# A streaming encoder layer whose second half reuses weight parts that the first half has made, and whose sample rows get a task of their own

## The chip, the cores and the metric

One core of one Trainium2 chip runs the whole kernel. Its engines have a queue each: TensorE (PE) does the matmuls, VectorE (DVE), ScalarE (ACT) and GpSimd (POOL) the work on elements, SyncE (SP) issues nearly all transfers (DMA). The time is the device time of one execution in microseconds, lower is better; several executions give the median. All times in this text come from one profiled execution and from the runs beside it.

## The reference

One layer for two request groups: 2048 prompt rows (new streams) and 32 sample rows (running streams), width 1024, all in float32. Cut to what matters here:

```python
h = rmsnorm(x, g_pre_mix); z = h @ w_in            # z: pool input u, and q, f, i, g of four heads
y_pool = pool_mix(u_ext, n_valid, w_pool, pool_scale)
S1, o = hgrn_run(S0, q, k, v, logf)                # recurrence by chunks
y_hg = rmsnorm(o, g_hg_norm) * silu(zg)
y_mix = concat([y_pool, y_hg]) @ w_out             # output projection
x = x + rmsnorm(y_mix, g_post_mix)
h2 = rmsnorm(x, g_pre_ffn)
f = (silu(h2 @ w_gate) * (h2 @ w_up)) @ w_down     # 1024 -> 2816 -> 1024
x = x + rmsnorm(f, g_post_ffn)
```

The outputs are both groups' rows and their new pool histories and recurrence states.

## The kernel before, in words

**A matmul.** An f32 matmul is done as three products of rounded parts: a tensor is split into `hi`, a rounded copy made by a cast on ACT, and `lo`, the rest, made by a subtraction on DVE; hi·hi, hi·lo and lo·hi are added up in PSUM. On top of this the projections work in 2x2 blocks with seven products of sums of blocks instead of eight (`PRODUCTS`, p = 1 to 7). The sums of blocks of a weight and their splits are its "forms".

**Stages.** The prompt is worked in two halves of 1024 tokens (`S.B` false and true). For each: values and front (norm, `w_in`, heads and pool), output projection (`project`), gate and up (`gate_up`), which writes the hidden rows to DRAM. `down` runs for both halves at the end. In the profiled execution the first half's front lasts until about 290 us, its projection until 374, its gate and up until 798; the second half's values until 842, front until about 1045, projection until 1141, gate and up until 1597, `down` until 2033.

**Weights of the projection.** A stream of items (`want`, `take`, L295 to L313) loads raw rows of 1024 numbers a partition (`wrow`, 512 KB) and splits each into two `whi` and two `wlo` tiles (L269, L270). `project` takes one item of two k-blocks at a time; its seven products run in the order of `PROJ`. The blocks for products 1, 2 and 3 are rows of `mixed` or `w_out`, those for 4, 5, 6 and 7 are sums that `out_forms` (L657) writes to DRAM, into `proj`, during the first half's front. Each half loads and splits all of them. The matmuls `ops` (stationary: tokens' forms `yhi`, `ylo`; moving: `whi`, `wlo`) end in a row tile `ym` per 128 tokens.

**From the projection to gate and up.** `finished` (L1530) sums the squares of half a row tile on ACT (`junk`, with a statistic in `st`; L343) and multiplies by the norm's weight on DVE (L1534). `post` (L1659) is a task for each group of four row tiles: POOL turns `st` into a reciprocal root (L347 to L354), DVE scales and adds the residual (L1693), ACT sums squares again (`junk`, 1024 wide), POOL makes a second root, the tile is scaled on DVE (L1676) or ACT (L1674), PE transposes it in quarters (`tps`, L366), and DVE and ACT take the transposes out of PSUM as `h2raw` (L373 to L377), from which `fhi` and `flo`, the tokens' forms, are made. The group of products 5 and 6 is the first, that of 2 and 3 the second. In the second half the second group has a fifth member, the 32 sample rows: matmuls `osps`, gathered into `yms` on ACT and DVE, multiplied by the norm's weight on POOL (L1578), and transposed last (`stps`, L420).

**Gate and up.** 22 column blocks of 256, `m` even for gate and odd for up. Each has seven forms `wf` (512 KB: hi and lo of 128x512) made from raw columns `wraw` (512 KB): `prep_sum`, `prep_hi` (ACT, L1847), `prep_lo` (DVE, L1852). The first six blocks (`LEAD`) are worked together product by product, in slots, since the second group of tokens is not ready at once. Both halves make all forms. The outputs in PSUM are `gx`, `gy`, `gz` and `gw`; `c` are their copies on the way to the hidden rows `hhi` and `hlo`.

**What sets the order.** PE's order is that in which the program is written. `Pace` counts the time of the matmuls written so far; a `Task` is a generator whose `yield n` says how many ns of matmuls are to pass before its next step, and `poll()` between matmuls takes the steps that are due. So the second group of transposes falls among the matmuls of gate and up where `post` is due. On DVE, ACT, POOL and SP a scheduler sets the order from its own estimate of what is ready; each of these queues is then worked strictly in that order. Tiles come from rings: 39 of 4 KB a partition (`wf`, `wraw`, `wrow`, `ym`, ...), 26 of 2 KB (`whi`, `wlo`, `c`, ...), and 8 PSUM banks, so a transfer or a matmul can also wait for the last reader of a buffer. `weight_forms` (L479) is a task that makes forms for the second half's front; what it has left is finished at the start of that half (`second_start`, L2298), ahead of its loads of `xT` and `wrow`.

## Time and profile before

| | us |
|---|---|
| median of 3 runs | 2042.76 (2042.34 to 2043.32) |
| profiled execution | 2042.75 |
| its span, first to last instruction | 2041.0 |
| PE busy | 2020.8 (99%) |
| DVE busy | 1522.4 (75%) |
| ACT busy | 900.9 (44%) |
| POOL busy | 274.1 (13%) |
| moved by DMA | 393 MB, mean 193 GB/s |

The span's mean granted clock of TensorE was 0.997. In a row of a timeline stand the start, the duration, the engine, the line, the operation and its tiles (out<-in), and in brackets the engine's idle time before it with what ended it. A matmul's duration overlaps the next one; what it costs is its distance to the next. A window row gives the stretch, its length, the busy time (and instructions) of PE, weight loads, DVE, ACT and POOL, the granted clock, the DMA engines' busy share and GB/s. A row of a group gives least, median and greatest duration in ns, and the first and last start in us.

### The profile page before, as it was taken

The page shows a single profiled execution, that of the slowest core. Times are in us where ns is not written, and L with a number is a line of the kernel's source. Part 1 is how long each engine was busy: PE and PEld are TensorE (multiplying, and loading weights), DVE is VectorE, ACT ScalarE, POOL GpSimd, SP SyncE. Part 2 cuts the span into 40 slices and gives each one's busy share as a digit, 9 for nine tenths or more (in the row PEclk, how much of TensorE's full clock was granted, in tenths as well). Part 3 has the DMA queues.
Part 4 walks back from the last instruction along what each step waited for, and adds up shares of the span by engine and source line. Part 5 has one row for each costly group of instructions (what it writes and reads, how often), then busy time and mean ns, then how long its engine had stood idle before and what let it go on. Part 6 is the DMA issues. An engine that isn't in the chain of part 4 may idle for free.

```text
span 2041.0 us, 34566 instructions
## 1 busy us (share of the span) xinstructions
PE 2020.8 (99%) x12892; PEld 1655.8 (81%) x12892; DVE 1522.4 (75%) x2515; ACT 900.9 (44%) x1800; POOL 274.1 (13%) x378
## 2 busy tenths in 40 slices
PE   9999999999999999999999999999999999999998
PEld 8888888788888888788887688888888778888876
DVE  5667678999788889666878887776676656566587
ACT  6654445864545445444456754444444411011032
POOL 0122311300000000033312300000001111010034
PEclk9999999999999999999999999999999999999999
DMA  8556333548776778745545615544455897677778
GB/s 296 181 187 218 115 113 135 186 130 250 227 238 212 228 222 253 264 160 176 168 177 180 188 53 155 165 145 144 141 149 160 252 355 215 204 228 206 216 202 217
DMA packets 434583, 393.33 MB, mean 193 GB/s; under 512 B 22680, under 2 KB 329360, under 8 KB 434416
## 3 DMA queue, kind: packets, MB, share of 16 engines
q1 hardware_dynamic: 427744, 381.11, 59.1%
q0 software_dynamic: 2016, 7.34, 2.0%
q10 hardware_dynamic: 4656, 2.67, 0.4%
q8 instruction: 102, 1.67, 0.3%
q14 instruction: 65, 0.53, 0.1%
HBM read 253.87 MB, written 137.17 MB: 192 GB/s over the span
## 4 chain that ended last, share of the span: by engine, by line
PE 90%; DVE 5%; ACT 1%; DMA 1%; POOL 1%; issue 1%; DVEq 0%; SPq 0%; ACTq 0%; POOLq 0%
PE gx L226 26%; PE gy L226 14%; PE dx L226 10%; PE mmb L226 8%; PE ops L226 6%; PE gz L226 6%; PE dy L226 5%; PE vps L226 4%; PE dz L226 3%; PE gb L226 1%; PE gw L226 1%; PE gsps L226 1%; DVE acc L2144 1%; PE ups L226 1%; DMA wraw<-in_w_up_dram 1%
## 5 line engine op out<-in xcount | busy, mean ns | idle before, releaser
L226 PE MATMUL gx<-fhi,wf 128*128 128x512 f32 x1632 | 459.5, 391 | 0.9 <-ACT c L1041 0.9
L226 PEld LDWEIGHTS gx<-fhi,wf 128*128 128x128 f32 x1632 | 304.6, 188 | 67.3 <-issue 1.6
L226 PE MATMUL gx<-flo,wf 128*128 128x512 f32 x816 | 255.3, 391 | 0.0
L226 PE MATMUL gy<-fhi,wf 128*128 128x512 f32 x832 | 239.7, 390 | 0.1
L226 PE MATMUL dx<-dhi,hst 128*128 128x512 f32 x640 | 185.4, 391 | 0.7 <-DVE acc L2144 0.7
L226 PEld LDWEIGHTS gy<-fhi,wf 128*128 128x128 f32 x832 | 155.5, 188 | 33.4 <-issue 0.9
L226 PEld LDWEIGHTS gx<-flo,wf 128*128 128x128 f32 x816 | 153.2, 188 | 31.9 <-issue 0.2
L2144 DVE TENSOR_TENSOR acc<-dx,acc 128x512 f32<-128x512 f32 x168 | 115.1, 689 | 71.4 <-PE dx L226 70.7
L1852 DVE TENSOR_TENSOR wf<-s,wf 128x512 fp32r<-128x512 f32 x176 | 120.4, 687 | 56.7 <-ACT wf L1847 55.7
L226 PEld LDWEIGHTS dx<-dhi,hst 128*128 128x128 f32 x640 | 119.6, 188 | 30.0 <-issue 3.4
L1847 ACT CAST wf<-s 128x512 fp32r<-128x512 f32 x176 | 107.7, 620 | 72.3 <-PE gy L226 27.9
L2083 ACT CAST dhi<-t 128x1024 fp32r<-128x1024 f32 x20 | 20.7, 1053 | 252.2 <-DVE dlo L2084 183.2
L226 PE MATMUL gy<-flo,wf 128*128 128x512 f32 x416 | 129.2, 390 | 0.0
L226 PE MATMUL gz<-fhi,wf 128*128 128x512 f32 x384 | 111.9, 392 | 1.0 <-ACT h2raw L375 1.0
L1847 ACT CAST wf<-wraw 128x512 fp32r<-128x512 f32 x132 | 80.7, 621 | 68.5 <-PE gx L226 38.8
L1852 DVE TENSOR_TENSOR wf<-wraw,wf 128x512 fp32r<-128x512 f32 x132 | 91.0, 694 | 18.6 <-ACT wf L1847 18.4
L226 PE MATMUL dx<-dlo,hst 128*128 128x512 f32 x320 | 98.7, 389 | 0.0
L226 PE MATMUL dy<-dhi,hst 128*128 128x512 f32 x320 | 98.5, 389 | 0.0
L226 PEld LDWEIGHTS gy<-flo,wf 128*128 128x128 f32 x416 | 78.1, 188 | 16.2
L2144 DVE TENSOR_TENSOR acc<-dy,acc 128x512 f32<-128x512 f32 x88 | 60.6, 689 | 38.6 <-PE dy L226 38.0
L226 PE MATMUL mmb<-hTlo,whi 128*128 128x512 f32 x256 | 84.6, 398 | 0.0
L226 PEld LDWEIGHTS gz<-fhi,wf 128*128 128x128 f32 x384 | 71.3, 188 | 15.6 <-ACT h2raw L375 1.2
(418 smaller groups left out, 4075.9 us busy)
## 6 DMA issues: line engine op xcount, KB each, us to landing
hst<-hdFalse SPq DMA_DIRECT2D x140, 256.0 KB, 3.1
hst<-hdTrue SPq DMA_DIRECT2D x140, 256.0 KB, 4.2
wf<-wd SPq DMA_DIRECT2D x112, 256.0 KB, 4.9
wraw<-in_w_gate_dram SPq DMA_DIRECT2D x50, 512.0 KB, 4.9
wraw<-in_w_up_dram SPq DMA_DIRECT2D x50, 512.0 KB, 4.2
hdFalse<-hhi SPq DMA_DIRECT2D x77, 256.0 KB, 2.6
hdFalse<-hlo SPq DMA_DIRECT2D x77, 256.0 KB, 2.5
hdTrue<-hhi SPq DMA_DIRECT2D x77, 256.0 KB, 2.3
```

Of the source, the lines that this page charges most:

```text
L226: nc.tensor.matmul(out, l, r, start=start, stop=stop, skip_group_check=more)
L1847: nc.scalar.copy(wf[:, 0], getattr(M, src) if isinstance(src, str) else src)
L1852: nc.vector.tensor_tensor(wf[:, 1], getattr(M, src) if isinstance(src, str) else src, wf[:, 0].bitcast(F32), ALU.subtract)
L2083: nc.scalar.copy(hi, src)
L2144: nc.vector.tensor_tensor(dst, ps, dst, ALU.add)
```

## The change

**Parts of the projection's weights.** `out_forms` now also splits: for each of four k-blocks and each of seven products, `put` casts the block or sum to `poh` on ACT and subtracts to `pol` on DVE, and stores both in DRAM (`proj`, 56 stores of 256 KB where there were 16). Both halves load them as `phi` and `plo` (`project_loads`, `project_take`), 56 + 56 loads of 256 KB each into the ring of 2 KB tiles, in place of 16 loads of 512 KB with 28 + 28 splits. The sample's projection loads its raw rows by itself.

**Kept forms.** The forms of gate and up of the first four blocks, and products 1 and 2 of blocks 4 and 5, 32 in all (`kept`), are stored by the first half when PE reaches their step (32 stores of 512 KB into `gd`), and the second half loads them into `wf` (32 loads) and neither sums nor splits. The raw columns that the sample's gate and up need are loaded when product 6 is prepared.

**The sample's own task.** `sample_post` takes the sample rows out of `post`: PSUM is copied once by ACT (`oss`), and the gathering, norms and transposes follow in a task of their own that begins 6000 ns of matmuls behind product 3 (`SAMPLE`). `post` has four members in both halves. The multiplication by the norm's weight moves from POOL to DVE.

**Later weights for the second front.** `weight_forms` begins 62000 instead of 50000 ns behind the projection.

```diff
+SAMPLE = 6000.0
+KEPT = 4
@@ project_loads @@
-        def project_loads(S):
-            def load(p, k):
...
-            for p in PROJ:
-                for k in pair_order(p):
-                    want(lambda p=p, k=k: load(p, k))
+        def project_loads(S, n):
+            forms_of_out.finish()
+            todo = [(p, k) for p in PROJ for k in pair_order(p)]
+            while len(S.pw) < min(n, len(todo)):
+                p, k = todo[len(S.pw)]
+                hl = [[t2("phi", dt=F32R), t2("plo", dt=F32R)] for _ in range(2)]
+                for kk in range(2):
+                    for i in range(2):
+                        nc.sync.dma_start(out=hl[kk][i].bitcast(F32), in_=proj[p][k + kk, :, i, :])
+                S.pw.append(hl)
+        def project_take(S, look):
+            i = S.pu
+            S.pu += 1
+            project_loads(S, i + 1 + look)
+            r = S.pw[i]
...
@@ out_forms, for each k @@
+                def put(p, src):
+                    hi, lo = t2("poh", dt=F32R), t2("pol", dt=F32R)
+                    nc.scalar.copy(hi, src)
+                    yield 2200.0
+                    v.tensor_tensor(lo, src, hi.bitcast(F32), ALU.subtract)
+                    for i, t in enumerate((hi, lo)):
+                        nc.sync.dma_start(out=proj[p][k, :, i, :], in_=t.bitcast(F32))
+                yield from put(1, b11)
+                yield from put(2, b21)
+                yield from put(3, b22)
...
-                for p, t in ((7, t3), (5, b12), (6, b22), (4, b21)):
-                    nc.sync.dma_start(out=proj[p][k * P:(k + 1) * P, :], in_=t)
+                yield from put(4, b21)
@@ project @@
                 def fetch(k, look):
-                    raw, hi, lo = take(look)
...
+                    w[k], w[k + 1] = project_take(S, look)
...
-                    S.post.append(Task(post(S, 1, yms[1], yss, sts[1]), 0.0, after=S.post[0]))
+                    S.post.append(Task(post(S, 1, yms[1], sts[1]), 0.0, after=S.post[0]))
                 if smp:
                     sample(p - 2, raws)
+                    if p == 3:
+                        S.post.append(Task(sample_post(S, yss, *rows), SAMPLE))
...
+        def sample_post(S, halves, xh, gv):
+            v = nc.vector
+            ym = [t2("yms", [NS, 512]) for _ in range(2)]
+            st = new_stat()
+            for i in range(2):
+                nc.scalar.copy(ym[i], halves[i][0:NS])
+                for q in range(1, 4):
+                    v.tensor_tensor(ym[i], halves[i][32 * q:32 * q + 32], ym[i], ALU.add)
+                sumsq(ym[i], NS, st[0:NS, i:i + 1])
+                yield 2500.0
...
+            for i in range(2):
+                v.tensor_tensor(ym[i], ym[i], gv[i], ALU.mult)
+                v.scalar_tensor_tensor(ym[i], ym[i], rs, xh[i][0:NS], ALU.mult, ALU.add)
+                nc.sync.dma_start(out=x1_rows(SEQ, NS)[:, i * 512:i * 512 + 512], in_=ym[i])
+                sumsq(ym[i], NS, st[0:NS, i:i + 1])
+                yield 2500.0
...
@@ gate_up @@
+                if S.B and m < KEPT:
+                    M.formed.update((0, 1))
+            def kept(m, p):
+                return m < KEPT or m < LEAD and p < 3
@@ load, prep_sum, prep_lo @@
+                if S.B and kept(m, p):
+                    return
@@ prep_hi @@
                 wf = M.f[p] = xtile("wf", [P, 2, 512])
+                if S.B and kept(m, p):
+                    nc.sync.dma_start(out=wf.bitcast(F32), in_=gd[m][p - 1])
+                    if p == 6:
+                        M.r = [raw_cols(M.w, (m // 2 * 2 + i) * P) for i in range(2)]
+                    return
@@ step @@
+                if kept(m, p) and not S.B:
+                    nc.sync.dma_start(out=gd[m][p - 1], in_=M.f[p].bitcast(F32))
@@ main @@
-                    forms = Task(weight_forms(), 50000.0)
+                    forms = Task(weight_forms(), 62000.0)
```

Three places where the order of instructions moves. The number behind a tile's name tells tiles apart; it is another in the two programs, and so are the line numbers.

DVE in the second half, ahead of the first group's transposes, before (row tiles of the first group: 11651, 11670, 11697, 11726; of the second: 11608, 11613, 11618):

```order
L1554 TENSOR_TENSOR ym_11608<-ops_12067,ym_11608 128x512
L1693 SCALAR_TENSOR_TENSOR ym_11726<-ym_11726,st_11506,xr_11882 128x512
L1693 SCALAR_TENSOR_TENSOR ym_11726<-ym_11726,st_11506,xr_11883 128x512
L1676 TENSOR_SCALAR ym_11651<-ym_11651,st_12054 128x1024
L1534 TENSOR_TENSOR ym_11608<-ym_11608,gv_11495 128x512
L1554 TENSOR_TENSOR ym_11613<-ops_12104,ym_11613 128x512
L270 TENSOR_TENSOR wlo_12141<-wrow_11987,whi_12140 128x512
L1554 TENSOR_TENSOR ym_11618<-ops_12148,ym_11618 128x512
```

and in the change (first group: 11811, 11830, 11855, 11874; second: 11760, 11765, 11770):

```order
L1566 TENSOR_TENSOR ym_11760<-ops_12214,ym_11760 128x512
L1730 SCALAR_TENSOR_TENSOR ym_11874<-ym_11874,st_11663,xr_12026 128x512
L1730 SCALAR_TENSOR_TENSOR ym_11874<-ym_11874,st_11663,xr_12027 128x512
L1546 TENSOR_TENSOR ym_11760<-ym_11760,gv_11652 128x512
L1714 TENSOR_SCALAR ym_11811<-ym_11811,st_12189 128x1024
L1566 TENSOR_TENSOR ym_11765<-ops_12251,ym_11765 128x512
L1566 TENSOR_TENSOR ym_11770<-ops_12295,ym_11770 128x512
```

The multiplication by `gv` of the second group's first tile has moved ahead of the scaling of the first group's first tile; the split is gone, and two additions out of PSUM follow the scaling at once. On ACT the sum of squares of that second group's tile now stands ahead of the scaling L1712, where it stood behind L1674.

PE at the start of the second half's gate and up, before (the second group's first transposes):

```order
L226 MATMUL gx_12538<-fhi_12321,wf_12413 128x512 x2
L226 MATMUL gx_12574<-fhi_12319,wf_12415 128x512 x2
L226 MATMUL gx_12574<-flo_12320,wf_12415 128x512 x2
L226 MATMUL gx_12574<-flo_12322,wf_12415 128x512
L366 MATMUL tps_12594<-cons_75,ym_11608 128x128
L366 MATMUL tps_12594<-cons_75,ym_11613 128x128
```

and in the change:

```order
L228 MATMUL gz_12627<-fhi_12494,wf_12536 128x512 x2
L228 MATMUL gx_12663<-fhi_12463,wf_12538 128x512 x2
L228 MATMUL gx_12663<-flo_12464,wf_12538 128x512 x2
L228 MATMUL gx_12663<-fhi_12465,wf_12538 128x512 x2
L228 MATMUL gx_12663<-flo_12466,wf_12538 128x512
L368 MATMUL tps_12692<-cons_75,ym_11760 128x128
L368 MATMUL tps_12692<-cons_75,ym_11765 128x128
```

The transposes have moved ahead by one product of 12 matmuls: they fall into the first `gx` behind the two `gz`, where they fell into the second. PE's order is the same everywhere else, but for the names of the projection's moving tiles.

ACT beside it, before:

```order
L1674 ACTIVATE ym_11613<-ym_11613,st_12483 128x1024
L343 ACTIVATE junk_12555,st_12554<-ym_11623 128x1024
L1847 CAST wf_12535<-wraw_12409 128x512
L1914 COPY c11_12565<-gx_12538 128x512
L1914 COPY c11_12611<-gx_12574 128x512
L1674 ACTIVATE ym_11623<-ym_11623,st_12554 128x1024
L1847 CAST wf_12571<-wraw_12407 128x512
L375 ACTIVATE h2raw2_12592<-tps_12604,cons_75 128x256 x2
```

and in the change:

```order
L1926 ACTIVATE c11_12560<-c11_12560 128x512
L345 ACTIVATE junk_12615,st_12610<-yms_12608 32x512
L345 ACTIVATE junk_12642,st_12641<-ym_11770 128x1024
L1712 ACTIVATE ym_11765<-ym_11765,st_12603 128x1024
L345 ACTIVATE junk_12651,st_12610<-yms_12609 32x512
L345 ACTIVATE junk_12671,st_12670<-ym_11775 128x1024
L1965 COPY c11_12709<-gx_12663 128x512
L345 ACTIVATE junk_12683,st_12679<-yms_12608 32x512
L345 ACTIVATE junk_12727,st_12679<-yms_12609 32x512
L377 ACTIVATE h2raw2_12690<-tps_12702,cons_75 128x256 x2
L1712 ACTIVATE ym_11775<-ym_11775,st_12670 128x1024
```

The casts `wf` are gone and sums of squares of the sample rows stand in their place; `h2raw2` has moved from behind the second scaling to ahead of it.

115 lines of the change are left out of this document (55 added, 60 removed).

## The prediction

> **What bounds the kernel now.** I read the page's first part, then the waits of TensorE (PE), then the windows and timelines around those waits.
>
> ```profile
> PE 2020.8 (99%) x12892; PEld 1655.8 (81%) x12892; DVE 1522.4 (75%) x2515; ACT 900.9 (44%) x1800; POOL 274.1 (13%) x378
> PE tps L366 <- ACT h2raw L375: 2.4, 1, 2.4
> PE tps L366 <- ACT ym L1674: 1.8, 2, 0.9
> PE tps L366 <- DVE ym L1554: 1.4, 2, 0.7
> PE gz L226 <- ACT h2raw L375: 1.0, 1, 1.0
> PE tps L366 <- DVE ym L1676: 0.8, 1, 0.8
> ```
>
> PE is busy for 99% of the span and the change keeps its 12892 matmuls. So removing work from VectorE (DVE) or ScalarE (ACT) shows in the time only where PE waits. The waits that the change can touch are these five, 7.4 us in all, around the transposes tps. The timelines say where they stand (PE rows of the two groups of the second half, then the first half):
>
> ```profile
> 1115.99 0.33 PE L366 MATMUL tps<-cons,ym 128*128 128x128 f32 x1 [0.80 <-DVE ym L1676]
> 1117.21 0.55 PE L366 MATMUL tps<-cons,ym 128*128 128x128 f32 x3 [0.89 <-ACT ym L1674]
> 1119.15 1.11 PE L366 MATMUL tps<-cons,ym 128*128 128x128 f32 x4 [0.70 <-DVE ym L1554]
> ...
> 1163.49 0.66 PE L366 MATMUL tps<-cons,ym 128*128 128x128 f32 x4 [2.40 <-ACT h2raw L375]
> 1166.93 0.74 PE L226 MATMUL gz<-fhi,wf 128*128 128x512 f32 x2 [0.96 <-ACT h2raw L375]
> ...
> 356.75 0.55 PE L366 MATMUL tps<-cons,ym 128*128 128x128 f32 x3 [0.89 <-ACT ym L1674]
> 358.69 0.66 PE L366 MATMUL tps<-cons,ym 128*128 128x128 f32 x4 [0.69 <-DVE ym L1554]
> ```
>
> One more loss is no wait. Windows of 4 us behind the first group (after the five busy times: granted clock, DMA share, GB/s):
>
> ```profile
> 1116.00:1120.00 4.00, 2.42 (x12) 1.74 (x12) 2.19 (x4) 3.96 (x9) 1.56 (x3) 0.80 0.94 304
> 1120.00:1124.00 4.00, 4.00 (x15) 3.21 (x14) 2.65 (x6) 2.92 (x7) 1.79 (x5) 0.50 0.83 270
> 1124.00:1128.00 4.00, 4.00 (x25) 1.67 (x24) 3.70 (x7) 3.27 (x7) 0.69 (x1) 0.84 1.12 357
> ```
>
> The clock stood at half for (0.20 + 0.50 + 0.16) x 4 / 0.5 = 6.9 us. With the 0.70 us in which PE waited anyway taken off, half of 6.2 us is lost: 3.1 us.
>
> **Output projection's parts, kept forms.** The projection's split leaves both halves:
>
> ```profile
> L269 ACT CAST whi<-wrow x56: 603/620/654, 275.7 to 1129.4; 128x512 fp32r<-128x512 f32 x56
> L270 DVE TENSOR_TENSOR wlo<-wrow,whi x56: 668/682/693, 278.4 to 1130.1; 128x512 fp32r<-128x512 f32 x56
> 75.00:270.00 195.00, 194.79 (x2532) 162.57 (x2531) 129.31 (x273) 94.93 (x278) 55.96 (x74) 1.00 0.50 167
> 1045.00:1130.00 85.00, 82.48 (x376) 65.61 (x375) 76.59 (x126) 52.37 (x106) 14.30 (x24) 0.96 0.54 189
> ```
>
> 28 casts of 0.620 (17.4 us of ACT) and 28 subtractions of 0.682 (19.1 us of DVE) leave each project stage; 28 of each, once, enter the first half's front (row 75 to 270), where DVE has 66 us and ACT 100 us free under a PE that is busy for 194.79 of 195. Cost there 0; without that cover 19 us. In the second project stage (row 1045 to 1130) DVE falls from 76.6 to about 57 us of 85. The 112 loads of 256 KB cost SP's queue; counted in matmuls each has at least 13 us from its buffer's release to its use, for a landing of 4.9 (wf<-wd, below): 0.
>
> The kept forms take 32 casts and 48 DVE operations out of the second half's gate and up, where PE shows no wait between 1176 and 1597: worth 0 by themselves. What they can cost is DMA.
>
> ```profile
> wf<-wd SPq DMA_DIRECT2D x112, 256.0 KB, 4.9
> wraw<-in_w_up_dram SPq DMA_DIRECT2D x50, 512.0 KB, 4.2
> 1170.00:1190.00 20.00, 20.00 (x96) 16.41 (x95) 19.64 (x25) 12.48 (x18) 0.00 (x0) 1.00 0.00 1
> 788.98 1.22 DVE L264 TENSOR_TENSOR wlw<-wrow,whw 128x1024 fp32r<-128x1024 f32 x1
> L226 PE MATMUL vps<-whw,fhi x64: 389/389/389, 798.5 to 840.9; 128*128 128x512 f32 x64
> ```
>
> A form of 512 KB that is loaded should land like wraw or wf<-wd, in 4.2 to 4.9 us. Counting 0.227 us a matmul in the order (42.4 us for the 187 from the first to the last of the vps row, the other products between them), all but two of the 32 loads have more than 10 us from the release of their buffer to their first matmul; two have 6.1. 6.1 less 4.9 and some 0.4 us of issue leaves 0.8, and the DMA engines rest before it (row 1170). Bounds 0 and 2 x 1 us; I take +0.5 for loads, since these two are the only ones near their limit.
>
> The later start of the second half's weights (62000 for 50000, 12 us) is made up at the stage's start. wlw is done 8.3 us ahead of vps; 12 us late would be a stall of 3.7. In the order it stands only some 3 us of matmuls later, so 0.
>
> **First group of transposes.** What is late is a chain, not a full engine (second half, DVE, ACT and POOL rows):
>
> ```profile
> 1115.19 0.75 DVE L1676 TENSOR_SCALAR ym<-ym,st 128x1024 f32<-128x1024 f32 x1
> 1117.81 0.69 DVE L1534 TENSOR_TENSOR ym<-ym,gv 128x512 f32<-128x512 f32 x1 [1.87 <-ACT junk L343]
> 1118.41 0.68 DVE L1554 TENSOR_TENSOR ym<-ops,ym 128x512 f32<-128x512 f32 x1
> ...
> 1116.01 1.15 ACT L1674 ACTIVATE ym<-ym,st 128x1024 f32<-128x1024 f32 x1 [3.15 <-POOL st L350]
> ...
> 1114.75 1.23 POOL L350 TENSOR_TENSOR st<-st,nhalf 128x1 f32<-128x1 f32 x1
> ```
>
> POOL's last statistic ends at 1115.98, ACT scales ym until 1117.16, and the first tile's four transposes need that. The statistics keep their order in the change and POOL has no less to do, so this wait stays: PE goes on at 1117.2. In the new order DVE multiplies the next ym by gv (0.6) ahead of the scaling, so the 0.80 becomes 1.4 and the 0.89 shrinks by as much: sum 0. The third wait goes. DVE's L1554, which frees the bank for the second tps, stood behind a multiplication that waited 1.87 us for ACT's junk, which itself stood behind ACT's ym. ACT's junk now runs before that ym and L1554 comes right behind the scaling, at 1116.5 instead of 1118.41, done at 1117.2, 1.2 us ahead of where PE stood (1118.45). Gain 0.7. In the first half the same order stands at 356 to 359: gain 0.7 again (the 0.69 row).
>
> The idle stretch behind which the clock fell shortens from 2.39 to 1.7 us. Two rows bracket that: in the first half 0.89 + 0.69 = 1.58 us, and in the second group 2.40 + 0.96 = 3.36 us, both passed without a drop. The new stretch is like the first half's, so I take the drop as gone: gain 3.1; the other end is 0.
>
> The Trainium skill ("TensorE: Matmul & The Clock Gate", section "Why this matters for your kernels") allows gaps up to about 3 us and drops to half only behind a whole idle window. By that rule no drop was due behind 0.80, 0.89 and 0.70; the trace disagrees (0.50 in the row of 1120). If only its rule held, the drop would have another cause and stay: the first rival.
>
> **Second group.** Its first transposes come 12 matmuls x 0.227 = 2.7 us earlier in PE's order (1154.5, for 1157.29), and the wf casts and wide yms steps of ACT and DVE that stood among the scalings are gone or later.
>
> ```profile
> 1149.35 1.07 PE L226 MATMUL gz<-fhi,wf 128*128 128x512 f32 x4
> ...
> 1153.73 0.63 ACT L1877 ACTIVATE c<-c 128x512 f32<-128x512 f32 x1 [0.76 <-DVE c L1921]
> 1154.26 1.04 ACT L343 ACTIVATE junk<-ym 128x1024 bf16<-128x1024 f32 x1
> ...
> 1161.04 1.15 ACT L1674 ACTIVATE ym<-ym,st 128x1024 f32<-128x1024 f32 x1 [1.02 <-POOL st L350]
> 1162.60 0.83 ACT L375 ACTIVATE h2raw<-tps,cons 128x256 f32<-128x256 f32 x2
> ...
> 1158.90 2.11 POOL L350 TENSOR_TENSOR st<-st,nhalf 128x1 f32<-128x1 f32 x1
> ```
>
> Before, h2raw (1162.60) stood behind ACT's ym (1161.04), which waited for POOL's 2.11 us. ACT's queue of the change, stepped by hand with these durations: DVE adds gz behind PE's 1149.8 and one yms addition, until 1150.8; activation 0.5 (1151.3); junk of yms 0.7; junk of ym 1.25 (1153.3); scaling 1.1: 1154.4, just in time for 1154.5. Then junk 0.7 and 1.25 (1156.3), copy 0.5, while POOL and DVE take st and yms until 1157.8; two junks of yms until 1158.6, two h2raw 0.8, scaling 1.1: 1160.5. PE needs that ym at 1154.5 + 4.8 = 1159.3. So 3.36 us of waits become about 1.2: gain 2.2. Bounds: gain 3.4 if POOL is quick, 0.2 if POOL takes its 2.11 on each of two statistics.
>
> **Sum.** 0.7 + 0.7 + 3.1 + 2.2 - 0.5 = 6.2 us off the profiled execution's 2042.75: 2036.5. The runs' median is 2042.76, so nothing is added.
>
> **Rivals.**
> 1. The clock still falls: the stretch is still 1.7 us long, and the drop came behind shorter single waits than the second group's 2.40. Against it: 1.58 us passed in the first half. 2036.5 + 3.1 = 2039.6. Chance 0.17.
> 2. The waits move rather than go: ACT's ym in the second group comes as late as before (POOL 2.11 again) and the clock falls too. 2042.75 - 1.4 + 0.5 = 2041.9. For it: POOL does the same work. Against it: two wf casts and the 32x1024 yms steps are gone from that stretch. Chance 0.10.
> 3. Slower: the stores of the forms crowd the loads in the first half's gate and up. DMA there (DMA share and GB/s end the window rows), and the page's GB/s by slices of 51 us:
>
> ```profile
> 365.00:475.00 110.00, 109.22 (x501) 89.41 (x500) 103.85 (x156) 72.61 (x124) 13.07 (x17) 1.00 0.53 162
> 465.00:475.00 10.00, 10.00 (x46) 8.29 (x45) 8.49 (x14) 4.29 (x8) 0.00 (x0) 1.00 0.85 253
> 394.78 0.69 DVE L1822 TENSOR_TENSOR s<-wraw 128x512 f32<-128x512 f32 x1 [1.98 <-DMA wraw<-in_w_up_dram]
> GB/s 296 181 187 218 115 113 135 186 130 250 227 238 212 228 222 253 264 160 176 168 177 180 188 53 155 165 145 144 141 149 160 252 355 215 204 228 206 216 202 217
> ```
>
> The 110 us move 162 GB/s x 110 us = 17.8 MB; 32 stores of 512 KB add 16.8, together 34.6 MB or 315 GB/s. DVE already waits 1.98 us for wraw there and is busy for 103.85 of 110. It decides if the queues hold less than 315: at the 253 of its last 10 us the bytes take 137 us instead of 110, and with half of these 27 us hidden by loads that run ahead PE loses some 13: 2036.5 + 13 = 2049.5. Against it: 355 GB/s held for a 51 us slice. Chance 0.12.
>
> **Chances and range.** The forecast has 0.61, with its own range 2033 (second group without a wait) to 2039. A change of 0.2% (4.1 us) is about what a measurement of this kernel can tell. Faster by that means under 2038.7: the forecast but for its top, 0.61. Within 0.2%: rivals 1 and 2 and that top, 0.27. Slower: 0.12, rival 3. The range, 2032 to 2044, holds the forecast and rivals 1 and 2 and leaves out rival 3 and a loss of more than 4 us on loads.
>
> **What would show it.** In the changed profile: no wait of tps on DVE ym L1566 near 358 and 1119; a wait on ACT ym L1712 still there near 1116; PEclk 1.00 from 1110 to 1130 of the new span; in the second group one wait of about 1 us on ACT ym, none on h2raw; no wait of gx or gz on DMA; DVE near 57 us in the second project stage. It is wrong if PEclk still shows 0.50, if gx or gy wait for wf, s or wraw between 370 and 480, or if the tps waits keep their 7 us.

## The result, and the profile after

The changed kernel takes 2048.59 us (median of 9 runs, 2043.32 to 2051.17) where the kernel before takes 2042.42 in the same comparison (9 runs, 2041.13 to 2044.17): a ratio of 1.0031 with the 95% interval 1.0021 to 1.0040. It is slower by 0.3%, and the forecast of 2036.5, with "faster" at 0.61, was wrong. The profiled execution took 2045.07 (span 2043.3, granted clock 0.999), at the low end of its runs, so the trace shows 2.3 us of a loss of some 6.

The page's first part and the waits of PE in the changed kernel (us in total, times, longest):

```profile
PE 2018.2 (99%) x12892; PEld 1654.2 (81%) x12892; DVE 1483.8 (73%) x2442; ACT 869.6 (43%) x1744; POOL 271.5 (13%) x377
PE ups L228 <- ACT kd L1404: 3.9, 4, 1.8
PE tps L368 <- DVE ym L1714: 1.5, 2, 1.1
```

DVE lost 38.6 us of work and ACT 31.3, and the time rose. The waits at the transposes shrank from 8.0 us (tps and gz, the small ones counted) to 4.8 in the whole program, as wanted; new is a wait of `ups` (the update of a head's state on PE) for `kd` (the operand that ACT copies for it) in the first half's front; it was 0.2 us before.

Stage by stage (from the first matmul of a stage to that of the next, worked out from each trace; the second half's projection is counted from the last `gy` of the front, some 3 us ahead of its own first matmul) the two profiled executions differ so:

| stage | before | after | predicted | measured |
|---|---|---|---|---|
| first half: values | 48.8 | 49.7 | 0 | +0.9 |
| front | 241.9 | 248.3 | 0 | **+6.4** |
| projection | 83.1 | 82.2 | -0.7 | -0.9 |
| gate and up | 424.8 | 427.6 | 0 | **+2.8** |
| second half: values and front | 247.8 | 248.4 | 0 | +0.6 |
| projection | 95.1 | 90.6 | -3.8 | -4.5 |
| gate and up | 455.3 | 452.7 | -1.7 | -2.6 |
| down | 435.9 | 435.3 | 0 | -0.6 |

(The second half's gate and up holds -2.2 for the second group and +0.5 for the loads of kept forms.) All the gains that were predicted are there. The loss comes from places that were priced at nothing.

**The gains.** PE's rows of the two groups of the second half, the window of 4 us behind the first of them, where the clock had been at half, and the project stage (it begins some 10 us later in the changed kernel, so both windows are taken later too):

```profile
1125.73 0.93 PE L368 MATMUL tps<-cons,ym 128*128 128x128 f32 x4 [1.11 <-DVE ym L1714]
...
1160.49 0.55 PE L368 MATMUL tps<-cons,ym 128*128 128x128 f32 x3 [0.28 <-ACT ym L1712]
...
1166.67 0.55 PE L368 MATMUL tps<-cons,ym 128*128 128x128 f32 x3 [0.73 <-ACT ym L1712]
```

```profile
1128.00:1132.00 4.00, 3.89 (x30) 1.94 (x28) 3.43 (x6) 3.97 (x10) 1.61 (x4) 1.00 0.96 328
1060.00:1145.00 85.00, 83.73 (x401) 67.37 (x399) 60.56 (x98) 42.29 (x87) 14.77 (x30) 1.00 0.82 286
```

Three waits of the first group (0.80, 0.89, 0.70) are one of 1.11, and the clock holds 1.00 where it was at 0.50. DVE is busy for 60.56 us of the 85, near the 57 that were forecast. DMA moves 286 GB/s for 189: 112 loads of 256 KB stand where the kernel before has 28 of 512 KB for the two projections (16 of them the sums in `proj`, the other 12 raw rows). In the second group 3.36 us of waits became 0.28 + 0.73, both on ACT's ym, none on h2raw.

**The loss.** The first half's front, the same 195 us as in the prediction, and PE's rows at the state update `ups` of three heads (first row: the kernel before; then the changed one):

```profile
209.04 0.71 PE L226 MATMUL ups<-va,kd 128*128 128x128 f32 x4 [0.21 <-ACT kd L1394]
```

```profile
75.00:270.00 195.00, 189.23 (x2493) 156.92 (x2492) 144.85 (x291) 105.85 (x289) 58.41 (x71) 1.00 0.62 213
163.78 0.71 PE L228 MATMUL ups<-va,kd 128*128 128x128 f32 x4 [0.61 <-ACT kd L1404]
214.43 0.71 PE L228 MATMUL ups<-va,kd 128*128 128x128 f32 x4 [1.85 <-ACT kd L1404]
265.64 0.71 PE L228 MATMUL ups<-va,kd 128*128 128x128 f32 x4 [1.25 <-ACT kd L1404]
```

PE is busy 189.23 us where it was 194.79, although DVE still has 50 us free and ACT 89. Why `kd` is late is seen in ACT's queue, which is worked in order. At the head of 163.78 the kernel before copies `kd` ahead of the eight copies into `attn`; the changed kernel has four of these copies and a cast `poh` of the new splits ahead of it, and they wait for DVE's masking `cmp` (ACT, the kernel before, then the changed one):

```profile
157.52 1.08 ACT L1394 COPY kd<-kps 128x512 f32<-128x512 f32 x2 [3.41 <-PE kps L1391]
158.74 1.73 ACT L1378 COPY attn<-gb 32x64 f32<-32x64 f32 x8
```

```profile
161.62 0.84 ACT L1388 COPY attn<-gb 32x64 f32<-32x64 f32 x4 [4.34 <-DVE cmp L1230]
162.50 0.62 ACT L673 CAST poh<-wo 128x512 fp32r<-128x512 f32 x1
163.14 0.58 ACT L1404 COPY kd<-kps 128x512 f32<-128x512 f32 x1
```

At the head of 265.64 the order of the two is the same in both kernels, and the copies wait longer for `cmp`: 4.78 and 1.01 us, where they waited 3.90 and 0.20. At the head of 214.43 other things delay `kd`; first the kernel before, then the changed one:

```profile
205.17 0.63 ACT L343 ACTIVATE junk<-xtl 128x512 bf16<-128x512 f32 x1 [2.48 <-DMA xtl<-in_x_prompt_dram]
205.92 1.71 ACT L1378 COPY attn<-gb 32x64 f32<-32x64 f32 x8
207.66 0.63 ACT L343 ACTIVATE junk<-xtl 128x512 bf16<-128x512 f32 x1
208.40 1.07 ACT L1394 COPY kd<-kps 128x512 f32<-128x512 f32 x2
```

```profile
209.06 0.63 ACT L345 ACTIVATE junk<-xtl 128x512 bf16<-128x512 f32 x1 [2.07 <-DMA xtl<-in_x_prompt_dram]
210.68 0.63 ACT L345 ACTIVATE junk<-xtl 128x512 bf16<-128x512 f32 x1 [0.90 <-DMA xtl<-in_x_prompt_dram]
211.43 1.71 ACT L1388 COPY attn<-gb 32x64 f32<-32x64 f32 x8
213.16 0.62 ACT L673 CAST poh<-wo 128x512 fp32r<-128x512 f32 x1
213.80 1.07 ACT L1404 COPY kd<-kps 128x512 f32<-128x512 f32 x2
```

PE's `kps`, which `kd` is copied from, starts at 209.50, and PE is ready for `kd` 3.1 us later (214.43 less the wait of 1.85). `kd` comes 4.30 us behind `kps`, where it came 2.65 behind it before (208.40 less 205.75). Both kernels wait for a load of `xtl` (the input of later statistics of x) ahead of the copies. In the changed one the second sum of squares of `xtl`, with 0.90 us more of waiting, stands ahead of the copies too, and a cast `poh` stands ahead of `kd`. `cmp` stands behind subtractions `pol` here as well, but it had ended (210.61) when the copies started (211.43), so at this head it is not what `kd` waited for. This wait is also the least steady: two more profiles of the changed kernel (below) have 0.36 and 0.07 us at this head, while the other two waits come back as 0.61 and as 1.30 and 1.32.

So no engine is full, and an in-order queue has become late, at two heads by `cmp` and at one by `xtl` and a cast. The next rows are the changed kernel's ACT ahead of the `kd` of 265.64, then ACT's waits from 75 to 270 us in the kernel before and in the changed one:

```profile
260.22 0.85 ACT L1388 COPY attn<-gb 32x64 f32<-32x64 f32 x4 [4.78 <-DVE cmp L1230]
```

```profile
ACT attn L1378 <- DVE cmp L1220: 4.3, 3, 3.9
```

```profile
ACT attn L1388 <- DVE cmp L1230: 10.4, 4, 4.8
ACT junk L345 <- DMA xtl<-in_x_prompt_dram: 5.7, 5, 2.1
```

ACT stands idle for 6.1 us more behind `cmp`. Its waits for `xtl` are no larger than before in sum (7.3 us there).

**First half's gate and up.** In the changed kernel DVE and ACT wait for transfers there, and the transposes of the second group wait for DVE and ACT by 0.88 and 1.03 us (DVE, ACT, the PE row of the second wait, the stretch that the prediction priced):

```profile
401.55 0.69 DVE L1864 TENSOR_TENSOR s<-wraw 128x512 f32<-128x512 f32 x1 [2.84 <-DMA wraw<-in_w_up_dram]
398.57 1.16 ACT L1712 ACTIVATE ym<-ym,st 128x1024 f32<-128x1024 f32 x1 [3.07 <-DMA out_dram<-ym]
403.90 0.63 PE L368 MATMUL tps<-cons,ym 128*128 128x128 f32 x4 [1.03 <-DVE h2raw L375]
365.00:475.00 110.00, 107.83 (x503) 88.51 (x502) 100.20 (x151) 72.97 (x129) 14.97 (x23) 1.00 0.88 302
```

302 GB/s moved where it had been 162: the stores of the kept forms. ACT's scaling of a `ym` waited for the store of `ym`, and DVE's next `h2raw` (402.88) stood behind the sum that waited for `wraw`. At 795 us, near the end of this stage, `gx` waits another 1.6 us for DVE's `wf`.

### The profile page after: what moved, and what is told of

Read it like the earlier page. It is cut to its first block, busy times and chain, and to the rows that moved or that the text cites. A ratio compares the mean times of both kernels' runs of the same rounds, so it can differ in the third digit from the quotient of the medians.

```text
span 2043.3 us, 34845 instructions
## 1 busy us (share of the span) xinstructions
PE 2018.2 (99%) x12892; PEld 1654.2 (81%) x12892; DVE 1483.8 (73%) x2442; ACT 869.6 (43%) x1744; POOL 271.5 (13%) x377
## 4 chain that ended last, share of the span: by engine, by line
PE 84%; DVE 8%; DMA 3%; issue 2%; ACT 2%; POOL 1%; SPq 0%; DVEq 0%; ACTq 0%; POOLq 0%
PE gx L228 25%; PE gy L228 13%; PE dx L228 10%; PE ops L228 7%; PE gz L228 6%; PE dy L228 5%; PE mmb L228 5%; PE vps L228 4%; PE dz L228 3%; PE gw L228 1%; PE gsps L228 1%; DVE acc L2195 1%; PE gb L228 1%; DMA wb<-in_w_in_dram 1%; PE ups L228 1%
## 5 line engine op out<-in xcount | busy, mean ns | idle before, releaser
L1901 DVE TENSOR_TENSOR wf<-s,wf 128x512 fp32r<-128x512 f32 x160 | 109.1, 686 | 52.9 <-ACT wf L1894 52.0
L1894 ACT CAST wf<-s 128x512 fp32r<-128x512 f32 x160 | 98.3, 621 | 64.1 <-PE gy L228 19.7
L1894 ACT CAST wf<-wraw 128x512 fp32r<-128x512 f32 x116 | 71.2, 621 | 57.1 <-PE gx L228 28.7
L1901 DVE TENSOR_TENSOR wf<-wraw,wf 128x512 fp32r<-128x512 f32 x116 | 79.1, 686 | 21.9 <-ACT wf L1894 21.6
```

Of the source, the lines that this page charges most:

```text
L1894: nc.scalar.copy(wf[:, 0], getattr(M, src) if isinstance(src, str) else src)
L1901: nc.vector.tensor_tensor(wf[:, 1], getattr(M, src) if isinstance(src, str) else src, wf[:, 0].bitcast(F32), ALU.subtract)
```

## Experiments

Each kernel is compared with runs of the kernel before on the same chip; "front", "project" and so on are the stages of the table above, from the profiled execution. Behind a median stand the lowest and the highest time, then the ratio to the kernel before and its 95% interval. Cuts in code and rows are marked by dots.

### Once more, without an edit

> The changed kernel once more, unedited, for a second profile: its executions ran from 2043.3 to 2051.2, and the profiled one (2045.1) was among the fastest. Stage by stage its first half's front (mmb) took 248.5 us for 242.0 of before, its first gate and up 427.5 for 424.7. Theory F (the splits in the front, with their stores on SP's queue, make the state chain of the heads late, by an amount that differs from run to run): whatever this execution is above 2045.1 shows in the front, as waits of ups on ACT kd. Rival D (the 32 stores of forms crowd the loads in the first gate and up): it shows there, as waits of gx or tps, and the front stays within 1 us of 248.5.

> The changed kernel once more, unedited, for a third profile. If the executions near 2048 to 2051 differ from the two profiled ones (2045.1 and 2042.6, both at a mean clock of 0.999 against 0.997 or 0.998 in most of the timed ones) by stretches at half clock, a profile at 0.998 shows one, behind a wait of ups in the front or of tps; if the spread is of waits alone, a slow profile shows the same clock and longer waits.

2042.63 and 2043.60 us, one profiled execution each, clock 0.999; front 247.5 both times, gate and up 426.6 and 427.9, second project 90.5, second gate and up 452.7. The stages repeat within 1.3 us, and so do gains and losses. Both executions are again below the median of 2048.59, so they do not show what makes the longer ones longer.

### One piece left out or alone

Change without the projection's parts (kept forms, sample's task and later weights on the kernel before):

```diff
-                    w[k], w[k + 1] = project_take(S, look)
+                    raw, hi, lo = take(look)
```

> The projection's parts undone (both halves split again, nothing is split in the front); kept forms, the sample's task and the later weights stay. Theory F: the front is back at 242.0 us (+-0.5), the spread between executions falls to about that of before (3 us), the first gate and up keeps its +2.8, the second half's projection may get its waits and the half clock back (up to 3.9) while the second group of transposes keeps its gain (2.6): 2039 to 2043. Rival D: the front gains its 6.5 but the spread of 8 us stays, 2041 to 2049.

2041.53 (2039.22 to 2043.85), ratio 0.9995 [0.9986, 1.0004]. Front 241.6: the loss is gone. Second project 95.0, with the half clock at 1120 still there: its gain is gone too. Second gate and up 452.1.

Change without the kept forms:

```diff
-            def kept(m, p):
-                return m < KEPT or m < LEAD and p < 3
```

> The kept forms undone (no stores into gd, the second half forms all again); the split parts, the sample's task and the later weights stay. Theory F: the front stays at about 248.5 us or more, the spread stays, the first gate and up is back at 424.7: 2043 to 2050, median about 2046. Rival D: the spread goes and the median falls by 5 or more, to about 2043.

2049.00 (2045.74 to 2053.02), 1.0032 [1.0019, 1.0044]. Front 248.1; first gate and up 424.0, so the 2.8 us there belong to the kept forms, which add only their stores to that half; second gate and up 459.3, where tps waits 0.74 and 3.43 us for DVE's ym and the clock is at half for 3.4 us behind the second of these waits.

The sample's own task alone, on the kernel before:

```diff
+                        S.post.append(Task(sample_post(S, yss, *rows), SAMPLE))
```

> The kernel before with the sample's own task alone. Theory F with the transposes' chains as the prediction stepped them: the first gaps of the first group stay, the third goes only if the order of DVE came from the lighter queues (with the splits still there it need not), the second group loses its fifth member and 1 to 2 us of wait: 2040 to 2042. Rival: the second group's gain came from the missing casts of the kept forms; then no gain here, 2042 to 2043.

2045.73 (2044.35 to 2046.97), 1.0018 [1.0009, 1.0028]: slower when it stands alone. Front 241.6, second gate and up 460.3 (455.3 before). PE's waits from 1075 to 1597 us in this kernel:

```profile
PE tps L367 <- DVE ym L1700: 5.1, 3, 3.4
```

and its DVE ahead of that ym:

```profile
1160.60 0.67 DVE L1871 TENSOR_TENSOR wf<-wraw,wf 128x512 fp32r<-128x512 f32 x1
1161.20 0.68 DVE L1667 TENSOR_TENSOR yms<-yms,gvs 32x512 f32<-32x512 f32 x1
1161.81 0.74 DVE L1700 TENSOR_SCALAR ym<-ym,st 128x1024 f32<-128x1024 f32 x1
```

The task's steps (`yms`) and the splits of gate and up (`wf`) stand ahead of the scaling that PE waits for; with the kept forms the second kind is gone.

The first group of this kernel has the same three waits as in the kernel before, but the clock does not fall behind them (PE, and the window of 4 us in which it had been at 0.50):

```profile
1116.44 0.33 PE L367 MATMUL tps<-cons,ym 128*128 128x128 f32 x1 [0.80 <-DVE ym L1700]
1117.65 0.55 PE L367 MATMUL tps<-cons,ym 128*128 128x128 f32 x3 [0.89 <-ACT ym L1698]
1119.60 0.66 PE L367 MATMUL tps<-cons,ym 128*128 128x128 f32 x4 [0.70 <-DVE ym L1548]
1120.00:1124.00 4.00, 3.67 (x29) 2.13 (x31) 4.00 (x9) 4.00 (x11) 2.15 (x6) 1.00 0.91 268
```

The second project takes 92.9 us here, where it took 95.1, with no wait of the first group removed.

Kept forms alone, on the kernel before:

```diff
+                if kept(m, p) and not S.B:
+                    nc.sync.dma_start(out=gd[m][p - 1], in_=M.f[p].bitcast(F32))
...
+                if S.B and kept(m, p):
+                    nc.sync.dma_start(out=wf.bitcast(F32), in_=gd[m][p - 1])
```

> The kernel before with the kept forms alone (the sample stays a fifth member of the second group). From e2 (kept forms and sample's task) and e4 (the task alone): first gate and up 426 to 427 (the stores), second gate and up. If the missing casts are what helped the second group: 452 to 453, whole 2040.5 to 2042. If it takes both the missing casts and the task: 455 or more, whole 2043 or more.

2039.07 (2037.79 to 2040.78), 0.9983 [0.9974, 0.9992]: faster than both kernels, by 0.17%. First gate and up 427.3 (+2.5), second 451.2 (-4.1), the rest as before, the half clock at 1120 included. PE's waits from 1075 us to 1597 are only those of the first group:

```profile
PE tps L367 <- ACT ym L1676: 0.9, 1, 0.9
PE tps L367 <- DVE ym L1678: 0.8, 1, 0.8
PE tps L367 <- DVE ym L1556: 0.7, 1, 0.7
```

All 3.36 us of the second group are gone without the sample's task. It was the forms' casts and subtractions between the scalings that made that group late.

The projection's parts alone, and with the kept forms:

```diff
+                yield from put(1, b11)
+                yield from put(2, b21)
...
+                    w[k], w[k + 1] = project_take(S, look)
```

> The kernel before with the projection's parts alone (split in the first half's front, loaded by both halves). By stages: front +6 us, first project -1, second project -4, second gate and up 0 to +4 (455 to 459): whole 2044 to 2049. Rival (the parts are worth it by themselves and the sample's task is what makes the change slower): 2042 or less.

> The kernel before with the kept forms and the projection's parts, without the sample's own task. If the pieces add by their stages: front of the first half 248, second half's project 91 to 92, second gate and up 451 to 453, whole 2039 to 2045 in the profile. Rival (the sample's task carries part of the second project's gain): second project 94 or more, and the whole 2045 to 2048.

Alone 2044.45 (2041.94 to 2048.92), 1.0015 [1.0006, 1.0025]: front 248.7, second project 93.3, second gate and up 455.7. Its first group has two waits, 1.11 and 1.41, and the clock is at half for 3.4 us behind them. With the kept forms 2043.60 (2040.49 to 2045.73), 1.0008 [0.9999, 1.0017], not to be told from the kernel before: front 249.8, second project 90.5, second gate and up 451.2. The parts lose more in the front than they gain in both projects, also without the sample's task.

### Which operation costs the front its 6 us

The changed kernel without the new casts and subtractions (both stores write the unsplit block):

```diff
-                    nc.scalar.copy(hi, src)
-                    v.tensor_tensor(lo, src, hi.bitcast(F32), ALU.subtract)
```

> The changed kernel without the 28 casts and 28 subtractions in the first half's front: each block or sum is stored twice as it is, so all 56 stores and all loads stay, in their places, and the projection computes with unrounded parts (hi and lo both the whole number, so its output is not the reference's). Theory W (ACT and DVE work in the front makes kd late for ups): the front falls from 248 to about 242, the median from 2048.6 to about 2042. Rival Q (the stores, on SP's queue and the DMA engines, make it late): the front stays at 246 or more and the median at 2046 or more.

2041.15 (2038.44 to 2046.04), 1.0000 [0.9991, 1.0010]; front 244.1. Stores and loads stay, and the ratio falls from 1.0031 to 1.0000, some 6 us; the profiled front falls by 4.2. The 2.2 us by which it is still longer than before are one wait of PE, behind a wait of ACT for `xtl` of 4.43 us, with neither a cast nor a subtraction in the front. Then the casts alone and the subtractions alone:

```diff
-                    v.tensor_tensor(lo, src, hi.bitcast(F32), ALU.subtract)
-                    for i, t in enumerate((hi, lo)):
-                        nc.sync.dma_start(out=proj[p][k, :, i, :], in_=t.bitcast(F32))
+                    for i in range(2):
+                        nc.sync.dma_start(out=proj[p][k, :, i, :], in_=hi.bitcast(F32))
```

> The changed kernel with the 28 casts of the front but without its 28 subtractions: the cast is stored twice, all stores and loads stay (hi and lo are both the rounded number, so the output is not the reference's). The state chain runs PE kps, ACT kd, PE ups; ahead of kd on ACT stand the copies attn, which wait for DVE's cmp, and in the change two casts poh. Theory A (ACT's casts ahead of kd): front 247 to 248, median 2047 or more. Theory V (DVE's subtractions ahead of cmp, so attn and kd come late): front at 244 as without both, median about 2041. Half each if both.

```diff
-                    nc.scalar.copy(hi, src)
-                    v.tensor_tensor(lo, src, hi.bitcast(F32), ALU.subtract)
+                    v.tensor_tensor(lo, src, src, ALU.subtract)
```

> The mirror of e9: no cast in the front, 28 subtractions of a block from itself, and the block and the result stored (hi is the unrounded block, lo is zero, so the output is not the reference's to the last bits). Theory V: front 247 to 248, median 2047 or more. Theory A: front 244, median about 2041.

Casts alone: 2040.53 (2039.20 to 2043.93), 0.9993 [0.9983, 1.0002], front 242.6. Subtractions alone: 2047.48 (2044.20 to 2051.17), 1.0026 [1.0017, 1.0036], front 249.8. The stretch of 195 us with casts alone, then with subtractions alone, and PE's waits in the latter:

```profile
75.00:270.00 195.00, 194.59 (x2529) 162.13 (x2528) 129.31 (x274) 108.45 (x300) 55.78 (x74) 1.00 0.62 215
```

```profile
75.00:270.00 195.00, 189.45 (x2481) 157.03 (x2480) 143.75 (x288) 91.51 (x261) 58.26 (x71) 0.99 0.62 213
PE ups L228 <- ACT kd L1403: 4.1, 3, 2.6
```

The casts make ACT busier (108.45 against 94.93) and PE loses nothing; the subtractions leave ACT below that and PE loses 5 us, most of them in waits for ACT's `kd`. The engine that PE waits for is not the one that got too much. DMA moves the same 213 to 215 GB/s in both, so the stores are not it either. Some 1.7 us of the front of 249.8 are clock: it is at half for 3.4 us behind the wait of 2.56 at 213.9.

The load of xtl some 6 us of matmuls further ahead of its use:

```diff
-                yield 6000.0
+                yield 12000.0
...
-                yield 14000.0
+                yield 8000.0
```

> All of the change, with the loads xtl of the second half's statistics 12 us instead of 6 ahead of ACT's junk, which in the front waits for them at the head of ACT's queue (2.07 and 0.90 us just ahead of kd at 209 us). If that wait is what makes kd late: front 246 or less, median 2045 or less. If the casts and subtractions alone do it: front 247.5 to 248.3, median 2047 to 2050.

2044.18 (2042.10 to 2050.17), 1.0011 [1.0002, 1.0021]; profiled front 249.4. The median is what the first reading expected, the profiled front is above what either did. ACT's waits and PE's from 75 to 270 us in it:

```profile
ACT attn L1388 <- DVE cmp L1230: 12.4, 5, 4.8
ACT junk L345 <- DMA xtl<-in_x_prompt_dram: 0.6, 2, 0.3
PE lv L228 <- issue: 2.3, 1, 2.3
PE ups L228 <- ACT kd L1404: 2.1, 3, 1.3
```

With the load's wait down from 5.7 to 0.6, the wait for `kd` falls from 3.9 to 2.1 (at the second head nothing of it is left) and the wait for `cmp` stays. So the late load is a part of the loss; how much, one profile does not tell. A new stall of 2.3 us that nothing in the trace explains, and a clock at half for 3.4 us behind it, some 4 us together, hide the gain in the profiled front.

### The same subtractions elsewhere

On GpSimd, in the same place, in the changed kernel and in the kernel with kept forms and parts:

```diff
-                    v.tensor_tensor(lo, src, hi.bitcast(F32), ALU.subtract)
+                    nc.gpsimd.tensor_tensor(lo, src, hi.bitcast(F32), ALU.subtract)
```

> Theory V (VectorE's queue in the first half's front is what the 28 subtractions cost: each stands ahead of the copies of cmp that the state chain waits for): with the same 28 subtractions on GpSimd, some 1.3 us each by its row for 128x512, the first half's front comes back to 242 to 244 us (248.3 in the change), TensorE's waits for kd in it fall under 1 us, and the whole is 2039 to 2042. Rival (the cost is the number of operations or bytes in the front, whichever engine makes them, or GpSimd's own copies into attn are now late in its place): the front stays at 246 or over, with the wait for kd or attn still there and now behind GpSimd, and the whole is 2045 or more.

> As the run before it, with the front's 28 subtractions on GpSimd. Theory V: front of the first half 242 to 244, second project 91 to 92, second gate and up 451 to 453, whole 2034 to 2038, below both kernels and below the kept forms alone (2039). Rival: front 246 or over and the whole 2040 or more.

2055.21 (2049.43 to 2060.11), 1.0064 [1.0043, 1.0085], and 2052.30 (2050.86 to 2053.88), 1.0053 [1.0036, 1.0070]. That GpSimd would free VectorE's queue is refuted. The front takes 259.6 us in the first of the two and 257.2 in the second, the project 82.1 and 82.0 as in the changed kernel. POOL, DVE and PE's waits in the first of them from 48 to 300 us (the DVE line has a mean of 721 ns over 30 in the changed kernel):

```profile
L675 POOL TENSOR_TENSOR pol<-wo,poh 128x512 fp32r<-128x512 f32 x28 | 41.4, 1492 | 13.9 <-ACT poh L673 12.4 <-issue 1.3
L272 DVE TENSOR_TENSOR wlo<-wraw,whi 128x512 fp32r<-128x512 f32 x30 | 26.7, 905 | 1.0 <-ACT whi L271 1.0
PE ups L228 <- ACT kd L1404: 5.2, 3, 2.9
PE kps L1401 <- DVE k_t L1189: 2.5, 2, 1.4
```

GpSimd makes products k_t of the heads as well, DVE itself is slowed, and PE waits for DVE's `k_t` (2.5 us) and `qa` (3.8) as well as for `kd`. GpSimd has no room on the head's chain either. Another 3.4 us of that front are clock, at half for 6.8 us behind the wait of 2.85 at 220.

In the first half's project, whose splits are made there anyway, and only stored for the second half; then the same with `KEPT = 0` (12 of the 32 forms kept):

```diff
+                        for i, x in enumerate(w[k + kk]):
+                            nc.sync.dma_start(out=parts[p][k + kk, :, i, :], in_=x.bitcast(F32))
```

> All of the change, but the parts are not made in the front: the first half loads and splits in its projection as the kernel before does, and stores what it has split (56 stores of 256 KB there); the second half loads these parts as in the change. Theory W: front 242, first projection 83.1 to 84, second projection 90.6 with no half clock, second gate and up 452.7, first gate and up 427: profile about 2037.5, median 2036 to 2041, spread under 5. Rival Q': the stores in the projection delay its loads and its chain, first projection 85 or more; then 2040 to 2044.

> As e6, but only products 1 and 2 of the first six blocks are kept (12 stores and 12 loads of 512 KB for 32). Theory: the second group's transposes fall among these products, so the second gate and up keeps its gain (452 to 454 us, against 459.3 with no form kept), and with 20 stores fewer the first gate and up is back at about 425: 1 to 2 us faster than e6. Rival: the gain of the second group needs the later forms too; then the second gate and up is at 455 or more.

2045.04 (2042.95 to 2052.22), 1.0024 [1.0015, 1.0033], and 2052.57 (2048.50 to 2054.18), 1.0054 [1.0042, 1.0067]. The front is as before (241.8 and 242.2) and the second project 90.6 and 90.8, but the first project takes 87.9 and 89.1 for 83.1. The first gate and up grows as well, to 431.2 and 428.3: it begins with a wait of 3.3 us for ACT's `fhi` and 6.8 us at half clock behind it. With fewer kept forms the second gate and up takes 458.7.

Last, a task of its own that makes the parts for the second half in the first gate and up, with kept forms and without the sample's task; one block each 15 us, then each 9 us of matmuls and from 20 us earlier:

```diff
+                    part_task = Task(part_forms(), 130000.0)
...
+                    hi, lo = t2("poh", dt=F32R), t2("pol", dt=F32R)
+                    nc.scalar.copy(hi, src)
+                    nc.vector.tensor_tensor(lo, src, hi.bitcast(F32), ALU.subtract)
```

> The kernel before with the kept forms; its first half splits the projection's weights in its own project as before, and a task of its own makes the parts for the second half, one 128x512 block each 15 us from about 130 us into the first gate and up (28 more loads, casts, subtractions, 56 more stores); the second half loads them. If it is the place of the subtractions that costs (the state chain of the first half's front), the front stays at 242, the second project falls to 91, first gate and up stays within 3 us of 427, and the whole is 2034 to 2038, under the kept forms alone (2039). Rival (the 28 blocks cost VectorE or the queues their 6 us wherever they are made): 2041 to 2047, with the loss in the first gate and up or the second half's front.

> As the run before it, with the 28 blocks 10 us apart from 110 us on, so that all fall into the first gate and up and none into the second half's front. If the place is what costs (18 of the 28 subtractions fell into the first gate and up in the run before, whose stage did not grow, 427.5 after 427.3; the 10 others fell into the second half's values and front, which grew by 5.4): second half's front 204 to 205, second project 90.5, first gate and up 427 to 429, whole 2034.5 to 2037.5. Rival (the first gate and up has no room for the closer pace, by its DMA share of 0.85 to 0.92 in the run before): gate and up 431 or more and the whole 2039 or more.

2042.20 (2040.37 to 2044.81), 1.0005 [0.9995, 1.0014], and 2043.66 (2041.54 to 2045.13), 1.0006 [0.9997, 1.0015]. Both expectations of a gain failed. In the first, 17 of the 28 blocks were split in gate and up, which took 427.5 us (427.3 with the kept forms alone), and 11 in the second half's values and front, where the front took 209.8 (204.4). In the second, all lay before 807 us: front 205.5, but gate and up 434.5, with one wait and half clock behind it near its end (PE's row, and a window of 4 us):

```profile
794.51 1.22 PE L227 MATMUL gy<-fhi,wf 128*128 128x512 f32 x2 [3.23 <-ACT c L2010]
```

```profile
794.00:798.00 4.00, 3.49 (x8) 2.81 (x9) 4.00 (x6) 3.53 (x7) 0.00 (x0) 0.50 0.60 199
```

So gate and up hid 17 splits at no price, and neither front hid the splits that it was given. What the closer pace costs is not shown. The clock was also at half for 3.4 us at 398, over 100 us ahead of the first block; ACT's `c` of the wait above stood behind a sum that waited for DVE, and no split of a part stands in either queue in the 7 us before; and the medians of the two runs do not differ beyond their intervals. Of all versions run, the kept forms alone are the fastest.

## Why the prediction was wrong, point by point

1. **The first group** (-0.7 in each half): right. The third wait is gone in both halves. "Sum 0" for the other two was cautious: 1.69 us became 1.11. But the wait that was to stay, for ACT's ym near 1116, is the one that went; the 1.11 us are for DVE's ym.
2. **The clock** (-3.1): right in the profile, for a reason that does not hold, so partly by luck. The forecast bracketed a stretch of 1.7 us between two that had passed; what came was a single wait of 1.11, and behind a single wait of 1.11 or 1.12 at that place no profile shows a drop. But the three waits do not decide: the sample's task alone has all three and keeps its clock, the kernel before and the kernels with kept forms and no parts have them and lose it. So the 3.1 us were not lost for certain in every execution of the kernel before, and the parts are not sure to save them: with the parts alone the clock still fell, for 3.4 us. Rival 1 did not happen, rival 2 neither.
3. **The second group** (-2.2): right in size (-2.6 with the loads, whose +0.5 was not seen: PE shows no wait for `wf<-gd`, `phi` or `plo`). Its origin was half understood: I named the casts that leave and the sample's steps that leave. The kept forms alone take all of it away; the sample's task alone makes that stage 5 us longer. The queue stepped by hand also gave two sums of `yms` 0.4 us each where it had counted 0.7 for the first (they took some 0.75); with 0.7 the gain would have been 1.6. "Worth 0 by themselves", said of the kept forms because PE shows no wait between 1176 and 1597, left out that the forms' work also stood at 1157 to 1167.
4. **The front** ("Cost there 0; without that cover 19 us."): this is the step that failed. It took 66 us of free DVE and 100 us of free ACT in 195 us for cover. Shown: with the subtractions that front takes 6 to 8 us more, with the casts alone 0.7. What counts there is the slack of one chain, PE's kps, ACT's kd, PE's ups, and of what stands ahead of kd in ACT's queue, and the kernel before already showed that it was nil: 0.2 us of PE waiting for kd, in the list of waits that I read, and ACT's attn waiting for cmp up to 3.9 us. The question to ask was which instruction of the new order stands ahead of kd or cmp, and it could be asked of the order before any run: at one head four copies that wait for cmp, and a cast, had moved ahead of kd.
5. **The stores of the kept forms** (0, and 13 as rival 3): the mechanism of rival 3 was right and its size wrong. The loads do wait (2.84 us for wraw), that stage took 426.6 us or more in every kernel that keeps four blocks, and 424.0 to 424.8 without kept forms. The rate held 302 GB/s in those 110 us, near the 315 asked for, where 13 us supposed 253. This term was put at 0 in the sum and cost 2.8 us.
6. **The sum.** The steps that were forecast (stages of both projects and the second gate and up) give -8.0 where -6.2 were predicted; front and first gate and up give +9.2 and the rest +0.9, which makes 2.1 of the 2.3 us of the profiled execution. The timed executions lose some 3.5 us beyond that, and the cause of this part stays open. Two more profiled ones (2042.63, 2043.60) had clocks of 0.999; the timed ones had 0.999 to 0.997. 0.001 of the mean clock is about 2 us of a 2043 us span, so the clock may be where part of it lies. The three profiles of the changed kernel have no half clock ahead of 2035 us, but three kernels near it have one of 3.4 us in this front, behind waits of PE (the subtractions alone at 215, the earlier load of xtl at 207, kept forms and parts at 164). No longer execution of the changed kernel itself was profiled. The pieces do not add up either: kept forms and parts are at 1.0008, and the sample's task with the later weights makes that 1.0031 in the timed runs, where the profile of its stages shows 1.5 us more in the second gate and up and 1.5 less in the front. How the 6 us divide between the late load of xtl and cmp stays open too.

## What to carry to other kernels

Free engine time summed over a stage is no cover for work that goes into an in-order queue: list what the new order puts ahead of the operations that the bounding engine already waits for, even where that wait is 0.2 us, and price the change by that chain. The 28 splits cost 6 us in a front of short dependent steps, and 17 of them nothing at a slow pace in a stage of long matmuls. When a change has several pieces, price and try each alone: of the three tried alone here (the later weights were not) one was a gain, and the sum was a loss.

## What the runs showed of the chip that was not expected

**Clock.** The waits of PE alone do not tell whether the clock falls. Behind the same three waits within 4 us (0.78 to 0.80, 0.89, and 0.69 or 0.70) it fell in the kernel before and with kept forms alone, and not with the sample's task alone (rows above). A wait of 2.40 passed in the kernel before, and behind one of 2.41 at the same place the clock fell with the parts alone. Single waits of 3.23 (rows above) and 3.42 (sample's task alone) were followed by a drop, and a single wait of 1.11 or 1.12 at the first group never was. In all profiles the drops ahead of 2025 us last some 3.4 or 6.8 us. A window of the kernel with kept forms alone, right behind its three waits:

```profile
1122.00:1126.00 4.00, 3.31 (x13) 2.87 (x13) 3.95 (x8) 4.00 (x11) 2.60 (x6) 0.50 0.87 261
```

The Trainium skill ("TensorE: Matmul & The Clock Gate", section "Why this matters for your kernels") asks for no gaps over about 3 us; the waits of 3.23 and 3.42 agree; the drops behind the three short ones, and behind single waits of 2.41 (parts alone) and 2.56 us (subtractions alone), do not.

**GpSimd beside VectorE.** The subtraction of 128x512 takes 1.49 us on GpSimd and 0.79 on DVE in that front, and in the kernel where GpSimd makes it, DVE's own subtractions of the same shape take 0.905 instead of 0.721 us on average. The Trainium skill ("SBUF — State Buffer", section "SBUF: two separate sides") describes one pair of ports that VectorE and GpSimd take in turn, each for a whole instruction; the slower DVE rows agree with that.
